# SiLU as one ScalarE operation in a hybrid attention, state-space and feed-forward layer

## The chip, the cores and the metric

The kernel runs on one core of a Trainium2 chip. The core has a matrix engine (TensorE, PE in the profile, with its weight loads shown as PEld), a vector engine (VectorE, DVE), a scalar engine (ScalarE, ACT), a general engine (GpSimd, POOL) and queues of transfers that SyncE (SP) starts. Each engine works through its own queue of instructions in order and waits where an instruction needs another engine's result or a free buffer. The metric is the time of one launch on the device, in microseconds (us), as the median of several runs.

## The reference

One layer of a decoder over 1024 positions of width 1024, all in float32. What matters here is where a sigmoid, and where a SiLU, silu(a) = a * sigmoid(a), is computed:

```python
h = rms_norm(x, g_pre_mix)
q, k, v, z, xbc, dt_raw, ga, gs = _split(h @ w_in, IN_SIZES)
o_att = stick_breaking_attention(q, k, v)      # beta = sigmoid(q.k / sqrt(d)), causal
...
xbc = silu(conv4(xbc) + conv_b)                # 3072 channels, 4 taps over time
xs, bm, cm = _split(xbc, (2048, 512, 512))
y = ssd_chunked(xs * dt, dt * a, bm, cm) + d_skip * xs
y = y * silu(z)                                # 2048 channels
...
merged = sigmoid(ga) * (o_att @ w_br_att) + sigmoid(gs) * (o_ssm @ w_br_ssm)
x = x + rms_norm(merged @ w_mix_out, g_post_mix)
...                                            # cross-attention into 256 memory tokens
gate, up = _split(h @ w_gu, (2816, 2816))
x = x + rms_norm((silu(gate) * up) @ w_down, g_post_ffn)
```

The SSD (state-space) part and the cross-attention use exponentials, `dt` a softplus by exponential and logarithm.

## The kernel before, in words

**Products.** Each operand of a matrix product is split into a high and a low part: ACT rounds the high part off (`hi_sb`, L97), VectorE subtracts it for the low part (`lo_of`, L100), and PE makes three matmuls (high by high, high by low, low by high: L103 to L105 in `mm3`, L223 to L225 in `acc3`). Weights come from memory by transfers (`wr`, `wraw`), are added to one another where the block schemes of Strassen and Winograd want sums (POOL, L199 to L202, `sf`), and are split into `sw`, which PE reads. A pair of column blocks takes seven such products in place of eight (`winograd_weights`, `winograd_pair`), their sums being formed in `y` by ACT and VectorE (L233 to L244, L710).

**Stages**, with the time in the profiled span at which each runs:

- 0 to 82 us: norm of `x`, first products of `v` and `z` (`v_out`, `z_out`).
- 82 to 272: the rest of `v` and `z` with positions on the partitions (`put_v`, `put_z`). In `put_z`, `zo` is the block of z that goes to memory; its sums `zk`, `zu`, `ma` are made at L613 to L621.
- 272 to 660: x, B and C with channels on the partitions, by pairs of 128-channel blocks (`pair`). For each block `conv` takes the first tap and the bias by one ACT operation (L668), the other three taps by VectorE (L670), then the SiLU (L671, L672), and `tail` turns the result by PE transposes (L660) that ACT copies out (L662). Pairs of merge gates (`gate`, a Sigmoid at L681) are strewn among the twelve pairs of `conv` by a sorted list, roughly one after every two.
- 640 to 1070: stick-breaking attention. ACT takes the Sigmoid of the scores (L881), VectorE scans them (L882), PE transposes (L898), ACT and VectorE split the weights (L901, L902).
- 1070 to 1410: SSD in chunks of 128 positions: a product gives the decays' exponents (`dec`, L1072), ACT their Exp (L1073), VectorE masks and multiplies them (L1074), PE multiplies by the chunk (`pd`, L1124, eight heads) and makes the states (`pst`), VectorE adds `pd` (L1127). Until about 1210 the keys and values of the memory are projected between the chunks (weights `wraw`, split into `bw`, products `mm` at L103 to L105).
- 1410 to 1880: branch projections, mix, cross-attention.
- 1880 to 1950: entry of the feed-forward: two blocks by plain products (`standard`), while VectorE makes the operands of the Strassen scheme (`combos`, L1748 to L1773).
- 1950 to 2310: the feed-forward's gate and up products in pairs; `gated` makes silu(gate) * up for 128 channels and 512 positions (Sigmoid L1728, product by the gate L1729, product by `up` L1730) and sends it to memory.
- 2310 to 2540: down projection and last norm.

**What sets the order.** The program is written as one function and run through a planner that lays every instruction on a simulated timeline (`schedule_with_timeline_sim=True`, L2051) and writes each engine's queue in the order that this timeline gives. An edit in one place thus changes the order in others. Tile pools give buffers in turn (nine for `sw`, six of PSUM, the matmul results' memory, in the convolution stage), and an instruction waits until its buffer's last reader is done. Function tables of ACT are not in the source: an ACT_TABLE_LOAD is put ahead of an activation whose function is not in the set loaded last. Sigmoid, Silu, Exp and Ln are in different sets in this program; Copy and Identity need no load.

Of the kernel before, what the change touches and what calls it, by code (L numbers as in the profile page):

```python
# [11 lines left out]
AF = mybir.ActivationFunctionType  # L12
ALU = mybir.AluOpType
# [22 lines left out]
def hybrid_block(ctx, tc, a, out, dbg=None):  # L36
    nc = tc.nc
    V, A, G, T = nc.vector, nc.scalar, nc.gpsimd, nc.tensor
# [11 lines left out]
    def mk(pl, shape, dt, tag, bufs=None):  # L50
        uid[0] += 1
        kw = {} if bufs is None else {"bufs": bufs}
        return pl.tile(shape, dt, tag=tag, name=f"{tag}_{uid[0]}", **kw)
# [87 lines left out]
    def pcol(nm, k):  # L141
        c = P + rows[nm] + k
        return prmT[:, c:c + 1]

    def cw(t, f):
        return prmT[:, t * 24 + f:t * 24 + f + 1]
# [107 lines left out]
    with ExitStack() as pa:  # L254
# [55 lines left out]
        with ExitStack() as p1:  # L310
# [87 lines left out]
                nc.sync.dma_start(v_d[1 + c * P:1 + (c + 1) * P, i * HALF:(i + 1) * HALF], to)  # L398

            def z_out(c, i, x, to):  # L400
                A.activation(to, x, AF.Sigmoid)
                V.tensor_tensor(to, x, to, ALU.mult)
                nc.sync.dma_start(zs_d[c * P:(c + 1) * P, i * HALF:(i + 1) * HALF], to)

            def u_kept(ps):
# [34 lines left out]

            load_v, steps_v = ahead(C_V, v_out, u_kept)
            load_z, steps_z = ahead(C_Z, z_out, u_away)
            normed(0)
            normed(1)
# [27 lines left out]
        with ExitStack() as p1:  # L472
# [11 lines left out]
            def put_z(c, i, x):  # L484
                if c % 2 == 0:
                    two["t"] = mk(op, [P, S], F32, "zo")
                sg = two["t"][:, c % 2 * HALF:(c % 2 + 1) * HALF]
                A.activation(sg, x, AF.Sigmoid)
                V.tensor_tensor(sg, x, sg, ALU.mult)
                nc.sync.dma_start(zs_d[c * P:(c + 1) * P, i * HALF:(i + 1) * HALF], sg)  # L490

            def put_v(c, i, x):
# [130 lines left out]

            token_major(0, C_V, put_v, 0, True)
            token_major(1, C_Z, put_z, 0, True, dt_chain())
            token_major(2, C_Z + 2 * HALF, put_z, 2)
        pz.close()

# [8 lines left out]
        with ExitStack() as p1:  # L637
# [28 lines left out]
            def conv(f, y):  # L666
                acc = mk(t4, [P, S], F32, "b4")
                A.activation(acc, y, AF.Identity, scale=cw(3, f), bias=pcol("conv_b", f))  # L668
                for sh in (1, 2, 3):
                    V.scalar_tensor_tensor(acc[:, sh:], y[:, :S - sh], cw(3 - sh, f), acc[:, sh:], ALU.mult, ALU.add)  # L670
                A.activation(y, acc, AF.Sigmoid)  # L671
                V.tensor_tensor(acc, acc, y, ALU.mult)  # L672
                if 16 <= f < 20:
                    nc.sync.dma_start(bf_d[f - 16], acc)
                if f >= 20:
                    nc.sync.dma_start(cf_d[f - 20], acc)
                else:
                    pend.append((f, acc))
# [24 lines left out]
            def pair(c0, f, fin, npool, beside=()):  # L703
# [9 lines left out]
                for h in beside:  # L713
                    differences(h)()

            jobs = [(C_X + f * P, f, conv) for f in list(range(16, 24, 2)) + list(range(0, 16, 2))]
            gts = [(C_GA + f * P, f, gate) for f in range(0, 16 - LATE_GATES, 2)]
            order = [(-(-(i + 0.5) / len(l)), n, j) for n, l in enumerate((jobs, gts)) for i, j in enumerate(l)]
# [255 lines left out]
    acc = []  # L974
# [505 lines left out]
    with ExitStack() as q2:  # L1480
# [28 lines left out]
        def cols(t, c):  # L1509
            return t[:, :, c * P:(c + 1) * P]  # L1510
# [27 lines left out]
        for c in range(4):  # L1538
            x, y, z = cols(d1, c), cols(q67, c), cols(q45, c)
# [177 lines left out]
    with ExitStack() as q4:  # L1717
# [7 lines left out]
        def gated(f, half, gate, up):  # L1725

            sg = mk(t2, [P, HALF], F32, "t2")
            A.activation(sg, gate, AF.Sigmoid)  # L1728
            V.tensor_tensor(sg, sg, gate, ALU.mult)  # L1729
            V.tensor_tensor(sg, sg, up, ALU.mult)  # L1730
            nc.sync.dma_start(gu_d[f * P:(f + 1) * P, half * HALF:(half + 1) * HALF], sg)

        def standard(f):
            ws = wgu if f == 0 else [wq_load(rp, "wr", colblock(w_gu, c0 + f * P)) for c0 in (0, FFN)]
            for half in range(2):
                gate, up = pre if f == half == 0 else [proj(w, hf[half]) for w in ws]
                gated(f, half, gate, up)
# [8 lines left out]
        def whole(pair, k, eng):  # L1746
            t = mk(t2, [P, HALF], F32, "t2")
            eng.tensor_tensor(t, pair[0][:, k, :].bitcast(F32), pair[1][:, k, :].bitcast(F32), ALU.add)  # L1748
            return t
# [21 lines left out]
        for k in range(4):  # L1771
            x21, x = whole(b21, k, V), whole(t2_, k, V)
# [5 lines left out]
        def strassen(f):  # L1778
            def loads(r, kh):
                for b in range(2):  # L1780
                    yield r[:, :, b], w_gu[kh * 512:(kh + 1) * 512, b * FFN + f * P:b * FFN + (f + 1) * P].rearrange("(k p) f -> p k f", p=P)

            y = [[mk(t2, [P, HALF], F32, "t2"), mk(t2, [P, HALF], F32, "t2")], [None, mk(t2, [P, HALF], F32, "t2")]]
            p = winograd_pair(psp, winograd_weights(rp, sfp, swp, loads), hw, y)
            gated(f, 0, y[0][0], p)
            gated(f, 1, y[0][1], y[1][1])
# [268 lines left out]
```

## Time and profile before

| what | value |
|---|---|
| median of 3 runs | 2538.93 us (2537.61 to 2540.65) |
| profiled execution, own time | 2542.52 us |
| profiled execution, span (first to last instruction) | 2540.8 us |
| instructions | 32839 |
| busy: PE, DVE, ACT, POOL | 97%, 73%, 46%, 31% |
| mean granted PE clock | 0.996 |
| ACT_TABLE_LOADs | 9, each 1.28 us |

How to read it: busy shares are means over the whole span. A group's row gives engine, line, operation, the names of result and operands with their shapes, a count, busy us and mean ns of one, and then how long its engine stood idle before such instructions and on what it waited ("<-DVE sw L100": until VectorE's instruction of line 100 that writes `sw` was done). A row of the timeline begins with the start and the duration in us. The time of an execution is a little above its span, since the span begins with its first instruction.

### The profile page before, as it was taken

To read this page: it belongs to the slowest core of one execution; us is meant where nothing else is said; L and a number is where in the kernel's file an instruction comes from. 1 tells how busy PE (TensorE), PEld (TensorE's weight loads), DVE (VectorE), ACT (ScalarE), POOL (GpSimd) and SP (SyncE) were. 2 spreads that over 40 slices of the span, in tenths; PEclk is the share of its full clock that TensorE was granted. 3 is DMA by queue.
4 is the path that set the end of the run, shared out by engine and by line. 5 is a ranking of instruction groups with operands and counts; after the bars stand their busy time and mean duration, and the time that the engine had idled before them with its cause. 6 is when DMAs were issued, how large, how long until landed. Compare 5 with 4: busy or idle time off the path is not lost.

```text
span 2540.8 us, 32839 instructions
## 1 busy us (share of the span) xinstructions
PE 2473.5 (97%) x12002; PEld 2053.7 (81%) x12002; DVE 1856.2 (73%) x2197; ACT 1156.7 (46%) x2071; POOL 791.5 (31%) x629
## 2 busy tenths in 40 slices
PE   7999999999999999998999999999999999999998
PEld 6788788888888888787888788887887888887776
DVE  7686878776688887687888654576458666666997
ACT  6343455655555555565554302344333333334433
POOL 4331533331000000165655231131123233233675
PEclk9999999999999999999999999999999999999999
DMA  6441565445454453464332452321131322324322
GB/s 229 150 152 61 153 200 182 137 139 158 116 129 113 118 128 103 143 207 152 102 94 81 160 162 87 121 90 64 62 121 59 97 78 75 99 84 166 133 100 100
DMA packets 285996, 311.59 MB, mean 123 GB/s; under 512 B 17407, under 2 KB 205960, under 8 KB 285450
## 3 DMA queue, kind: packets, MB, share of 16 engines
q1 hardware_dynamic: 285834, 309.49, 39.2%
q8 instruction: 95, 1.56, 0.2%
q14 instruction: 67, 0.55, 0.1%
HBM read 206.26 MB, written 78.52 MB: 112 GB/s over the span
## 4 chain that ended last, share of the span: by engine, by line
PE 42%; DVE 6%; issue 1%; POOL 1%; DMA 1%; ACT 1%; SPq 0%; POOLq 0%; DVEq 0%; ACTq 0%
PE mm L225 5%; PE mm L223 5%; PE mm L224 5%; PE mm L103 4%; PE mm L104 4%; PE mm L105 4%; DVE op L100 2%; PE p L103 2%; PE p L104 2%; PE p L105 2%; PE pd L1124 2%; DVE a L1931 1%; PE p L1639 1%; DMA gr<-gu_d 1%; PE tr L181 0%
## 5 line engine op out<-in xcount | busy, mean ns | idle before, releaser
L882 DVE TENSOR_TENSOR_SCAN n<-n,mask 128x128 f32<-128x128 f32 (+7 forms) x128 | 170.8, 1350 | 39.9 <-ACT n L881 39.4
L199 POOL TENSOR_TENSOR sf<-wr,wr 128x512 f32<-128x512 f32 x38 | 61.4, 1617 | 354.6 <-DMA wr<-in_w_gu_dram 105.5
L100 DVE TENSOR_TENSOR sw<-sf,sw 128x512 fp32r<-128x512 f32 x150 | 114.5, 775 | 55.1 <-ACT sw L97 54.7
L93 POOL TENSOR_SCALAR whi<-wraw 128x1024 fp32r<-128x1024 f32 x10 | 18.3, 1829 | 397.8 <-PE mm L104 324.7
L97 ACT ACTIVATE sw<-sf 128x512 fp32r<-128x512 f32 x150 | 92.0, 625 | 96.2 <-PE mm L225 85.7
L881 ACT ACTIVATE n<-sc 128x512 f32<-128x512 f32 (+1 forms) x192 | 86.8, 493 | 93.6 <-PE sc L880 93.1
L97 ACT ACTIVATE sw<-wr 128x512 fp32r<-128x512 f32 x113 | 70.9, 629 | 123.4 <-PE mm L225 123.3
L225 PE MATMUL mm<-h,sw 128*128 128x512 f32 x320 | 125.0, 392 | 1.8 <-DVE sw L100 1.8
L223 PE MATMUL mm<-h,sw 128*128 128x512 f32 x320 | 122.6, 391 | 3.1 <-ACT h L97 2.3
L224 PE MATMUL mm<-h,sw 128*128 128x512 f32 x320 | 125.2, 391 | 0.0
L166 POOL TENSOR_SCALAR rstd<-ms 128x1 f32<-128x1 f32 x82 | 31.5, 384 | 294.6 <-ACT x L1417 132.7
L902 DVE SCALAR_TENSOR_TENSOR wtl<-tr,wth 128x512 fp32r<-128x512 f32 x192 | 99.5, 545 | 29.8 <-ACT wth L901 29.4
L901 ACT ACTIVATE wth<-tr,mone 128x512 fp32r<-128x512 f32 x192 | 106.5, 582 | 23.9 <-PE tr L898 21.7
L670 DVE SCALAR_TENSOR_TENSOR b<-b,prmT,b 128x1023 f32<-128x1023 f32 (+2 forms) x72 | 102.2, 1420 | 9.8 <-ACT b L668 9.2
L100 DVE TENSOR_TENSOR sw<-wr,sw 128x512 fp32r<-128x512 f32 x113 | 93.7, 832 | 19.0 <-ACT sw L97 18.9
L103 PE MATMUL mm<-oth,bw 128*128 128x512 f32 x256 | 104.1, 407 | 1.5 <-DVE a L1183 1.4
L105 PE MATMUL mm<-oth,bw 128*128 128x512 f32 x256 | 101.4, 396 | 0.5 <-DVE bw L1170 0.5
L898 PE MATMUL tr<-ident,n 128*128 128x128 f32 x576 | 97.9, 275 | 3.4 <-DVE wtl L902 3.4
L104 PE MATMUL mm<-otl,bw 128*128 128x512 f32 x256 | 101.0, 394 | 0.0
L103 PE MATMUL p<-bw,h 128*128 128x512 f32 x256 | 99.7, 390 | 0.9 <-DVE m L1391 0.9
L100 DVE TENSOR_TENSOR zl<-zr,zh 128x512 fp32r<-128x512 f32 x84 | 75.4, 911 | 34.4 <-ACT zh L97 34.3
L105 PE MATMUL p<-bw,h 128*128 128x512 f32 x256 | 100.2, 392 | 0.0
(697 smaller groups left out, 8202.6 us busy)
## 6 DMA issues: line engine op xcount, KB each, us to landing
wr<-in_w_gu_dram SPq DMA_DIRECT2D x80, 256.0 KB
wr<-in_w_in_dram SPq DMA_DIRECT2D x36, 512.0 KB
zr<-in_w_in_dram SPq DMA_DIRECT2D x32, 512.0 KB
gu_d<-t SPq DMA_DIRECT2D x44, 256.0 KB
qk<-hT SPq DMA_DIRECT2D x84, 128.0 KB
qk<-lT SPq DMA_DIRECT2D x84, 128.0 KB
wraw<-in_w_in_dram SPq DMA_DIRECT2D x20, 512.0 KB
b<-v_d SPq DMA_DIRECT2D x16, 512.0 KB
```

Source lines behind the costliest of these rows:

```text
L97: A.activation(o, i, AF.Copy)
L100: eng.tensor_tensor(o, i, hi.bitcast(F32), ALU.subtract)
L103: first = T.matmul(ps, sh, mh, start=start, stop=False)
L104: T.matmul(ps, sh, ml, start=False, stop=False)
L105: T.matmul(ps, sl, mh, start=False, stop=stop)
L223: T.matmul(ps, w[0][:, k, :], b[0][:, k, :], start=first and k == 0, stop=False, skip_group_check=True)
L224: T.matmul(ps, w[0][:, k, :], b[1][:, k, :], start=False, stop=False, skip_group_check=True)
L225: T.matmul(ps, w[1][:, k, :], b[0][:, k, :], start=False, stop=last and k == 3, skip_group_check=True)
L670: V.scalar_tensor_tensor(acc[:, sh:], y[:, :S - sh], cw(3 - sh, f), acc[:, sh:], ALU.mult, ALU.add)
L882: V.tensor_tensor_scan(nt[:, 0:L][:, ::-1], nt[:, 0:L][:, ::-1], mask[:, S - L:][:, ::-1], 1.0, ALU.mult, ALU.max)
L901: A.activation(wh[:, t0 * P:], pt[:, t0 * P:], AF.Identity, bias=mone)
L902: V.scalar_tensor_tensor(wl[:, t0 * P:], pt[:, t0 * P:], -1.0, wh[:, t0 * P:].bitcast(F32), ALU.add, ALU.subtract)
```

## The change

In `z_out`, `put_z`, `conv` and `gated` the pair of Sigmoid on ACT and product on VectorE becomes one Silu on ACT. In `conv` the result goes into `acc` itself, and `y` is no longer written there.

```diff
             def z_out(c, i, x, to):
-                A.activation(to, x, AF.Sigmoid)
-                V.tensor_tensor(to, x, to, ALU.mult)
+                A.activation(to, x, AF.Silu)
                 nc.sync.dma_start(zs_d[c * P:(c + 1) * P, i * HALF:(i + 1) * HALF], to)
...
                 sg = two["t"][:, c % 2 * HALF:(c % 2 + 1) * HALF]
-                A.activation(sg, x, AF.Sigmoid)
-                V.tensor_tensor(sg, x, sg, ALU.mult)
+                A.activation(sg, x, AF.Silu)
                 nc.sync.dma_start(zs_d[c * P:(c + 1) * P, i * HALF:(i + 1) * HALF], sg)
...
                 for sh in (1, 2, 3):
                     V.scalar_tensor_tensor(acc[:, sh:], y[:, :S - sh], cw(3 - sh, f), acc[:, sh:], ALU.mult, ALU.add)
-                A.activation(y, acc, AF.Sigmoid)
-                V.tensor_tensor(acc, acc, y, ALU.mult)
+                A.activation(acc, acc, AF.Silu)
...
             sg = mk(t2, [P, HALF], F32, "t2")
-            A.activation(sg, gate, AF.Sigmoid)
-            V.tensor_tensor(sg, sg, gate, ALU.mult)
+            A.activation(sg, gate, AF.Silu)
             V.tensor_tensor(sg, sg, up, ALU.mult)
```

The other Sigmoids (`gate` L681, the late gates L858, the scores L881) stay. The changed file is shorter by a line at each place, so its line numbers are lower by one to four: L681 is L678, L671 is L669, L881 is L878, L1072 is L1069, L1124 is L1121, L1728 is L1725.

The queues change in three places that matter. First VectorE's queue between z and the convolution (about 270 us; `zu` are sums of z, `zo` the block of z that is sent, `sw` the split weights of the convolution's first pair). Before:

```order
L621 TENSOR_TENSOR zu_2044<-zu_2044,ma_2272 128x512
L621 TENSOR_TENSOR zu_2046<-zu_2046,ma_2273 128x512
L621 TENSOR_TENSOR zu_2048<-zu_2048,ma_2274 128x512
L489 TENSOR_TENSOR zo_2517<-zu_2044,zo_2517 128x512
L621 TENSOR_TENSOR zu_2050<-zu_2050,ma_2275 128x512
L489 TENSOR_TENSOR zo_2517<-zu_2046,zo_2517 128x512
L489 TENSOR_TENSOR zo_2526<-zu_2048,zo_2526 128x512
L100 TENSOR_TENSOR sw_2597<-wr_2582,sw_2597 128x512
L100 TENSOR_TENSOR sw_2598<-sf_2587,sw_2598 128x512
L489 TENSOR_TENSOR zo_2526<-zu_2050,zo_2526 128x512
```

And with the change:

```order
L619 TENSOR_TENSOR zu_2028<-zu_2028,ma_2252 128x512
L619 TENSOR_TENSOR zu_2030<-zu_2030,ma_2253 128x512
L619 TENSOR_TENSOR zu_2032<-zu_2032,ma_2254 128x512
L619 TENSOR_TENSOR zu_2034<-zu_2034,ma_2255 128x512
L100 TENSOR_TENSOR sw_2565<-wr_2550,sw_2565 128x512
L100 TENSOR_TENSOR sw_2566<-sf_2555,sw_2566 128x512
```

The products at L489 are gone, and the two splits follow the last sum directly.

Second, ACT's queue in the convolution stage, from a gate to the next convolved block (`b` are the blocks `y` and `acc`). Before:

```order
L681 ACTIVATE b_486_2760<-b_486_2760 128x1024
L97 ACTIVATE b_500_2902<-b_500_2902 128x8x64
L237 ACTIVATE b_515_2946<-mm_2948 128x512
L97 ACTIVATE sw_3076<-wr_3059 128x512
L97 ACTIVATE sw_3247<-wr_3235 128x512
L668 ACTIVATE b_520_3042<-b_515_2946,prmT_93 128x1024
L97 ACTIVATE sw_3248<-sf_3239 128x512
L97 ACTIVATE sw_3249<-sf_3240 128x512
L97 ACTIVATE sw_3250<-wr_3236 128x512
L671 ACTIVATE b_515_2946<-b_520_3042 128x1024
L97 ACTIVATE sw_3251<-sf_3241 128x512
```

And with the change:

```order
L678 ACTIVATE b_486_2726<-b_486_2726 128x1024
L237 ACTIVATE b_515_2912<-mm_2914 128x512
L97 ACTIVATE sw_3040<-wr_3023 128x512
L97 ACTIVATE sw_3209<-wr_3197 128x512
L666 ACTIVATE b_520_3008<-b_515_2912,prmT_93 128x1024
L97 ACTIVATE sw_3210<-sf_3201 128x512
L97 ACTIVATE sw_3211<-sf_3202 128x512
L97 ACTIVATE sw_3212<-wr_3198 128x512
L669 ACT_TABLE_LOAD
L669 ACTIVATE b_520_3008<-b_520_3008 128x1024
L97 ACTIVATE sw_3213<-sf_3203 128x512
```

A table load has come between the weight conversions and the SiLU of `conv`, and another stands ahead of the next pair of gates. In the whole program there are 21 loads in place of 9; eleven of the twelve new ones are of this kind, and one stands ahead of the first Sigmoid of the attention's scores.

Third, PE's queue near 1075 us, where the SSD's chunks and the memory's projections share PE (`dec` the decays, `pst` the states, `pd` the products with a chunk, `mm` the memory's products). Before:

```order
L1072 MATMUL dec_10338<-colrows_2076_10225,keyrows_2077_10226 128x512
L103 MATMUL mm_10369<-a_2073_10195,bw_10355 128x256
L104 MATMUL mm_10369<-a_2074_10196,bw_10355 128x256
L1072 MATMUL dec_10341<-colrows_2076_10225,keyrows_2077_10226 128x512
L103 MATMUL pst_10481<-s2r_10347,bh_10299 128x512
L104 MATMUL pst_10481<-s2r_10348,bh_10299 128x512
L105 MATMUL pst_10481<-s2r_10347,bl_10300 128x512
L105 MATMUL mm_10369<-a_2073_10195,bw_10355 128x256
```

And with the change:

```order
L1069 MATMUL dec_10282<-colrows_2076_10169,keyrows_2077_10170 128x512
L1069 MATMUL dec_10285<-colrows_2076_10169,keyrows_2077_10170 128x512
L1121 MATMUL pd_10460<-s_2102_10261,s_2103_10263 128x96 x6
L103 MATMUL pst_10425<-s2r_10291,bh_10243 128x512
L1121 MATMUL pd_10460<-s_2102_10261,s_2103_10263 128x96
L1121 MATMUL pd_10460<-s_2102_10261,s_2103_10263 128x64
L104 MATMUL pst_10425<-s2r_10292,bh_10243 128x512
L105 MATMUL pst_10425<-s2r_10291,bl_10244 128x512
L103 MATMUL mm_10313<-a_2073_10139,bw_10299 128x256
L104 MATMUL mm_10313<-a_2074_10140,bw_10299 128x256
```

The decays and the `pd` products of the first chunk now stand ahead of the first memory product; before, `pd` came behind the first 26 of the memory's matmuls. Further on the memory's products come in other blocks between the chunks than before.

## The prediction

> **What bounds the kernel now.** I read the busy shares first, then the same shares by stage, and then the waits inside the stages where the share falls. The page's first part:
>
> ```profile
> PE 2473.5 (97%) x12002; PEld 2053.7 (81%) x12002; DVE 1856.2 (73%) x2197; ACT 1156.7 (46%) x2071; POOL 791.5 (31%) x629
> ```
>
> TensorE (PE) works 2473.5 of the span's 2540.8 us. Whatever happens on VectorE (DVE) and ScalarE (ACT), no more than 2540.8 - 2473.5 = 67.3 us of PE idle time can be closed, beside time lost to a lowered clock. By stage (start and end, length, then busy us of PE, PEld, DVE, ACT and POOL, granted clock, DMA share, GB/s):
>
> ```profile
> 82.00:272.00 190.00, 189.82 (x835) 156.06 (x833) 129.78 (x183) 74.26 (x122) 50.90 (x26) 1.00 0.37 122
> 272.00:660.00 388.00, 382.87 (x1759) 315.53 (x1759) 302.29 (x316) 212.07 (x323) 119.10 (x74) 1.00 0.52 158
> 1070.00:1210.00 140.00, 123.19 (x727) 105.69 (x727) 113.37 (x122) 85.58 (x153) 79.80 (x69) 0.97 0.58 183
> 1880.00:1950.00 70.00, 65.22 (x273) 52.31 (x272) 62.02 (x79) 24.81 (x42) 26.14 (x15) 0.95 0.18 57
> 1950.00:2310.00 360.00, 359.22 (x1585) 297.25 (x1584) 230.20 (x269) 131.74 (x226) 106.91 (x68) 1.00 0.28 86
> ```
>
> The stages in which the change takes work from VectorE are 82 to 272 (z), 272 to 660 (convolution) and 1880 to 2310 (feed-forward). PE idles 0.2, 5.1, 4.8 and 0.8 us in the four rows that cover them. The 16.8 idle us of 1070 to 1210 hold no edited line.
>
> **What is removed.** A product and a Sigmoid become one Silu. The columns of a group are its count, then busy us and mean ns of one, then the engine's idle time before them and its releaser:
>
> ```profile
> L1729 DVE TENSOR_TENSOR t<-t,t 128x512 f32<-128x512 f32 x40 | 59.9, 1498 | 1.9 <-ACT t L1728 1.7
> L672 DVE TENSOR_TENSOR b<-b,b 128x1024 f32<-128x1024 f32 x24 | 37.1, 1546 | 4.9 <-ACT b L671 4.8
> L1730 DVE TENSOR_TENSOR t<-t,mm 128x512 f32<-128x512 f32 x24 | 16.5, 687 | 33.6 <-PE mm L225 31.3 <-PE mm L105 2.3
> L489 DVE TENSOR_TENSOR zo<-zk,zo 128x512 f32<-128x512 f32 x16 | 20.1, 1297 | 0.0
> L489 DVE TENSOR_TENSOR zo<-zu,zo 128x512 f32<-128x512 f32 x8 | 7.7, 996 | 0.0
> L489 DVE TENSOR_TENSOR zo<-ma,zo 128x512 f32<-128x512 f32 x4 | 2.7, 692 | 0.0
> L1729 DVE TENSOR_TENSOR t<-t,mm 128x512 f32<-128x512 f32 x4 | 2.7, 685 | 4.6 <-ACT t L1728 4.6
> L402 DVE TENSOR_TENSOR early<-ma,early 128x512 f32<-128x512 f32 x4 | 2.5, 684 | 0.6 <-ACT early L401 0.6
> ```
>
> Without L1730, which stays, these are 40+24+16+8+4+4+4 = 100 products and 59.9+37.1+20.1+7.7+2.7+2.7+2.5 = 132.7 us of VectorE, 7% of its work. L1730 shows why most of it buys nothing: the product by `up`, which follows L1729, has waited 33.6 us in all, nearly all for PE's matmuls. L1729 runs while PE is still making `up`.
>
> **What is added.** One ACT activation stands where one stood. No Silu is in this trace, so its duration is bounded by neighbours of the same size: a Sigmoid of 128x512 and a plain conversion.
>
> ```profile
> L1728 ACT ACTIVATE t<-t 128x512 f32<-128x512 f32 x40 | 25.3, 632 | 9.6 <-DVE t L244 3.9 <-DVE t L240 2.8
> L97 ACT ACTIVATE sw<-sf 128x512 fp32r<-128x512 f32 x150 | 92.0, 625 | 96.2 <-PE mm L225 85.7 <-POOL sf L200 4.4 <-POOL sf L202 2.4
> ```
>
> They differ by 7 ns, so I take no difference; the bound above is a Silu as dear as Sigmoid and conversion together, 0.63 us more apiece. In the feed-forward that is less than the L1729 that it replaces.
>
> Function tables are the second addition. The instruction order of the change holds 21 ACT_TABLE_LOADs, that of before 9. All 12 new ones lie in the convolution (11, because Silu of `conv` and Sigmoid of `gate` take turns) and at the first score of the attention (1). Their price:
>
> ```profile
> 462.01 1.28 ACT L671 ACT_TABLE_LOAD   x1 [0.51 <-DVE b L670]
> 463.30 1.06 ACT L671 ACTIVATE b<-b 128x1024 f32<-128x1024 f32 x1
> ```
>
> The activation starts 1.29 us after its load, so a switch costs 1.29 us of ACT, and it stands behind the wait for the data: the load does not run ahead of it. 12 x 1.29 = 15.5 us. The Trainium skill, page "ScalarE: Activation LUTs", sections "What ACT_TABLE_LOAD costs" and "Table sets: the hidden batching unit", tells authors to batch calls by table set and charges each switch a drain of about 1380 ns beside the load's 1283 ns, 2.66 us together. That rule speaks against this change. The row agrees on the load and shows no drain; by the page the twelve would be 31.9 us (an estimate from its figure), still ACT time.
>
> **The sum, place by place.**
>
> *z to convolution, 270 to 277 us.* VectorE's queue and PE's wait:
>
> ```profile
> 271.74 3.44 DVE L489 TENSOR_TENSOR zo<-zu,zo 128x512 f32<-128x512 f32 x2
> 275.10 1.76 DVE L100 TENSOR_TENSOR sw<-wr,sw 128x512 fp32r<-128x512 f32 x1
> 272.99 0.50 PE L225 MATMUL mm<-b11h,sw 128*128 128x512 f32 x1 [0.77 <-POOL sw L100]
> 276.92 0.50 PE L225 MATMUL mm<-b21h,sw 128*128 128x512 f32 x1 [1.36 <-DVE sw L100]
> ```
>
> Two z products, 3.44 us, stand directly ahead of the weight split for which PE waits 1.36 us. In the new order the four `zu` products are gone and the split moves up. The wait ends: **-1.4 us**. Bounds: 0 if the split finds its input late, -2.1 if the neighbour's 0.77 goes too.
>
> *Convolution.* What waits for what, in total us, times, and longest:
>
> ```profile
> PE tr L660 <- DVE b L672: 0.7, 2, 0.4
> ACT sw L97 <- PE mm L225: 42.2, 30, 5.4
> ACT b L710 <- PE mm L225: 38.9, 17, 4.1
> ACT b L671 <- DVE b L670: 21.5, 18, 4.5
> ```
>
> PE has waited 0.7 us for the removed product and so can win that much. The loads lengthen ACT by 11 x 1.29 = 14.2 us, to 226 of 388. Queued behind a load are weight conversions (L97), for which PE waits if they come late. But ACT itself idles for PE 42.2 + 38.9 us in this stage, so most loads end inside its slack. Each convolved block also loses a 1.55 us product and gains a 1.29 us load at most, so the transposes get their data no later. I take **0**; bounds -0.7 and +14.2 (no load covered).
>
> *First score of the attention.* One load stands ahead of it:
>
> ```profile
> 665.71 0.56 ACT L881 ACTIVATE n<-sc 128x128 f32<-128x128 f32 x2 [1.75 <-PE sc L880]
> 671.03 0.49 PE L898 MATMUL tr<-ident,n 128*128 128x128 f32 x3
> ```
>
> PE needs what comes of it 5.3 us later and multiplies other things until then: **0**, at most +1.29.
>
> *1070 to 1210.* No line here is edited, but the planner puts PE's queue in another order: four decays and eight `pd` products stand ahead of the first memory product, where they came after it. The largest waits:
>
> ```profile
> PE mm L103 <- ACT bw L97: 2.9, 1, 2.9
> PE po L104 <- DVE stl L100: 2.2, 1, 2.2
> PE pd L1124 <- DVE s L1127: 2.1, 3, 1.0
> PE dec L1072 <- ACT cb L1048: 2.1, 1, 2.1
> ```
>
> The new order puts work in front of the 2.9 us wait for memory weights, so that row could go. But eight `pd` products now come together, and the third row, their wait for the addition (L1127) that empties their buffer of the chunk before, could grow by as much. I take **0**. Bounds: -16.8 (all idle time of the stage) and +8.7 (a wait as long as the longest, 2.9, at each of the three places where the blocks of memory products are cut differently).
>
> *Entry of the feed-forward.* The only stretch where VectorE never rests:
>
> ```profile
> 1920.00:1930.00 10.00, 7.68 (x31) 5.95 (x30) 10.00 (x18) 4.17 (x8) 0.00 (x0) 0.92 0.03 8
> 1926.56 0.68 DVE L1729 TENSOR_TENSOR t<-t,mm 128x512 f32<-128x512 f32 x1
> 1926.76 0.50 PE L223 MATMUL mm<-h,sw 128*128 128x512 f32 x1 [2.31 <-ACT h L97]
> 1927.16 0.69 DVE L1759 TENSOR_TENSOR t<-t,t 128x512 f32<-128x512 f32 x1
> 1927.76 0.68 DVE L1729 TENSOR_TENSOR t<-t,mm 128x512 f32<-128x512 f32 x1
> 1930.00:1940.00 10.00, 8.01 (x28) 5.83 (x27) 10.00 (x18) 3.65 (x7) 2.45 (x1) 0.84 0.33 107
> 1937.53 0.50 PE L225 MATMUL mm<-h,sw 128*128 128x512 f32 x1 [1.82 <-DVE sw L100]
> ```
>
> Two L1729 stand in that queue ahead of the split for which PE waits 1.82 us. Each gives back one pitch, 1927.16 - 1926.56 = 0.60 us by their neighbours (L1729, then L1759, then L1729: 1.20 for two): **-1.2 us**. Bounds: 0 if the time goes to other operands, -4.1 if both waits (2.31 + 1.82) go, and up to 10 x (0.08 + 0.16) = 2.4 us more for the clock that fell behind them.
>
> *All else.* z at 82 to 272 and the feed-forward at 1950 to 2310 have PE busy in 189.82 of 190 and 359.22 of 360 us: **0**, with 0.2 + 0.8 = 1.0 us as the most that could be won. If that cover went, it would be the 132.7 us.
>
> Sum: -1.4 + 0 + 0 + 0 - 1.2 + 0 = -2.6 us on the profiled span of 2540.8. The profiled execution took 2542.5 in its own time, 1.7 more than its span, and lies 3.6 above the median of the runs, 2538.93. The difference carries over: 2538.9 - 2.6 = **2536.3 us**.
>
> **Rivals.**
>
> *A, the relief compounds.* The gap at the entry closes with its clock loss (-4.1 - 2.4), the transition gives 2.1, and the new order of 1070 to 1210 hides a quarter of its idle time (4.2): -12.8, or 2526. For it: the clock falls right behind the waits, and the 16.8 us lie in a region that is re-planned. Against it: nothing edited lies there. If only some of this comes, 2530.
>
> *B, the table switches decide.* Slower: 11 loads stand ahead of conversions that PE needs; the slack of ACT comes in pieces (42.2 us in 30 waits, 1.4 each, hardly more than one load), and an ACT that runs late makes PE wait by what is over. It decides once more than two loads' worth (2.6 us, the sum above) shows on PE, and is slower by more than 5.1 us once 6 of the 11 do. With 8 exposed: 2538.9 - 2.6 + 10.3 = 2547; all of them and the attention's: 2536.3 + 15.5 = 2552. Against it: ACT is busy 212 of 388 us. Charged as that page charges a switch, all twelve exposed would be 2568 (an estimate).
>
> *C, the new order costs.* Slower: the three places between 1070 and 1210 each gain a wait of 2.9 us: 2536.3 + 8.7 = 2545. For it: a planner's timeline is not the chip's. Against it: the stage has waits to lose too.
>
> *D, nothing.* PE's own order of work keeps the waits, each removed product's time going to the next operand in line: 2539.
>
> **How the numbers follow.** Forecast, small gain: 0.46. A 0.26, B 0.10, C 0.11, D 0.07. The forecast's own range is 2532 to 2540: its two gains at their bounds (-2.1 and -4.1, so 2532.7) and one exposed load above (2537.6), with some for the spread of the runs (2537.6 to 2540.7). The range of 8 in 10 takes in the middle of A, all of C and B up to eight exposed loads: 2525 to 2547; outside lie the far ends of A and of B. About 0.2%, or 5.1 us, is what a measurement can tell from no change: faster is below 2533.8, slower above 2544.0. A gives 0.24 of faster and the forecast's low end 0.06; B gives 0.09 and C 0.09 of slower; the rest is same, 0.52.
>
> **What would show each step.** In the changed profile: the wait of 1.36 us near 277 us gone; PE idle in 272 to 660 no more than 5.1 us with 11 loads in ACT's groups, each 1.28 us (B: new waits of PE on `sw` from ACT, about 1.3 us each); VectorE less by 120 to 133 us; PE busy unchanged near 2473; the stage 1950 to 2310 the same length; the waits at 1926 and 1937 us shorter by 1.2 in all. The forecast is wrong if the stage from convolution to attention grows by several us (B), or if 1070 to 1210 changes by more than 4 us either way (A or C): then the planner's order, and not the removed products, made the time.

## The result, and the profile after

The change takes 2531.97 us (median of 15 runs, 2528.16 to 2535.96) against 2538.93 for the kernel before (15 runs, 2536.68 to 2541.19): a ratio of 0.9972 with a 95% interval of 0.9966 to 0.9979, that is 5.3 to 8.6 us or 0.28% faster. The forecast was 2.6 us. The profiled execution took 2533.23 us, with a span of 2531.5.

The busy shares, from the page of the changed kernel:

```profile
PE 2471.4 (98%) x12002; PEld 2054.0 (81%) x12002; DVE 1745.0 (69%) x2097; ACT 1168.9 (46%) x2083; POOL 791.0 (31%) x629
```

A hundred instructions have left VectorE, and ACT has its twelve loads. TensorE's work is the same, so what was won is its idle time and its clock. The same stages as in the prediction, by time (columns as there; the last stages begin earlier now):

```profile
272.00:660.00 388.00, 384.42 (x1769) 317.63 (x1770) 265.32 (x289) 224.59 (x335) 113.56 (x74) 1.00 0.51 158
1070.00:1210.00 140.00, 127.82 (x754) 110.19 (x752) 115.28 (x125) 86.75 (x158) 78.93 (x72) 0.98 0.60 181
1880.00:1950.00 70.00, 67.24 (x287) 54.88 (x288) 60.50 (x80) 26.33 (x46) 38.11 (x15) 0.98 0.23 72
1950.00:2310.00 360.00, 359.22 (x1586) 297.11 (x1585) 189.46 (x227) 132.85 (x229) 104.02 (x67) 1.00 0.29 91
```

In the last row VectorE has 40.7 us less to do (230.20 before) and PE's 359.22 is unchanged to the hundredth: there the removed products were worth nothing. PE gains 1.6 us in the convolution, 4.6 from 1070 to 1210, and 2.0 at the entry of the feed-forward. Fixed windows shift against the work, though, so the stages are better cut at instructions that both kernels have. The entry runs from the last transposes of the normed stream to the first product of the Strassen scheme that uses `tx`. TensorE's timeline of before, and then of the change:

```profile
1884.97 1.03 PE L181 MATMUL tr<-ident,x 128*128 128x128 f32 x8
1949.71 0.39 PE L223 MATMUL mm<-tx,sw 128*128 128x512 f32 x1
```

```profile
1878.64 1.03 PE L181 MATMUL tr<-ident,x 128*128 128x128 f32 x8
1939.43 0.39 PE L223 MATMUL mm<-tx,sw 128*128 128x512 f32 x1
```

64.74 us have become 60.79: 3.95 us in this one place. The convolution stage, from its first product to the attention's first score, of before and of the change:

```profile
270.04 0.39 PE L223 MATMUL mm<-b11h,sw 128*128 128x512 f32 x1
665.22 0.39 PE L879 MATMUL sc<-qk 128*128 128x128 f32 x2
```

```profile
270.47 0.39 PE L223 MATMUL mm<-b11h,sw 128*128 128x512 f32 x1
663.60 0.39 PE L876 MATMUL sc<-qk 128*128 128x128 f32 x2
```

395.2 us have become 393.1. The SSD stage, cut in the same way (from the last attention product, `av`, to the last product of the state branch, `mm<-otl,bw`), went from 382.9 to 378.0; how much of that is the change's, the experiments have to say. These three cuts, in every kernel that was profiled (lengths in us, taken from the starts of the matmuls named; "entry" here from the last of the eight transposes):

| kernel | convolution | SSD | entry | ratio to before (95% interval) |
|---|---|---|---|---|
| before, the profile of the prediction | 395.2 | 382.9 | 64.0 | 1 |
| before, profiled again (e12) | 394.7 | 376.7 | 64.0 | 1 |
| the change | 393.1 | 378.0 | 60.0 | 0.9972 (0.9966 to 0.9979) |
| e1, last four z blocks | 395.2 | 375.6 | 62.6 | 0.9998 (0.9989 to 1.0007) |
| e2, the rest of z | 394.2 | 377.4 | 63.9 | 1.0000 (0.9991 to 1.0009) |
| e3, the change without the 11 switches | 393.1 | 376.9 | 60.0 | 0.9967 (0.9955 to 0.9980) |
| e4, feed-forward alone | 394.0 | 378.5 | 59.9 | 0.9985 (0.9977 to 0.9994) |
| e5, convolution alone | 394.8 | 382.9 | 63.9 | 1.0020 (1.0011 to 1.0028) |
| e6, z and convolution | 393.1 | 378.1 | 64.0 | 0.9993 (0.9984 to 1.0002) |
| e7, z and feed-forward | 395.8 | 376.3 | 60.6 | 0.9992 (0.9983 to 1.0000) |
| e8, first two feed-forward blocks alone | 394.2 | 377.3 | 59.3 | 0.9984 (0.9975 to 0.9993) |
| e9, the change, entry refilled | 393.3 | 377.9 | 64.0 | 0.9987 (0.9978 to 0.9996) |
| e10, the change, entry emptied further | 393.1 | 377.9 | 59.7 | 0.9970 (0.9959 to 0.9982) |
| e11, the change, 37 more loads | 404.0 | 376.9 | 60.6 | 1.0012 (1.0003 to 1.0020) |

0.001 of the ratio is 2.5 us. The lengths are those of one execution each, the ratio that of all runs. The profiled executions of e1 (2533.94 us) and e8 (2532.09) were the fastest of their eleven, and a stretch that no run edits, from the last product of gate and up to the end, lasted between 230.0 and 235.2 us.

### The profile page after: what moved, and what is told of

Same layout as the page of the kernel before. It is cut to its first block, busy times and chain, and to the rows that moved or that the text cites. A ratio compares the mean times of both kernels' runs of the same rounds, so it can differ in the third digit from the quotient of the medians.

```text
span 2531.5 us, 32776 instructions
## 1 busy us (share of the span) xinstructions
PE 2471.4 (98%) x12002; PEld 2054.0 (81%) x12002; DVE 1745.0 (69%) x2097; ACT 1168.9 (46%) x2083; POOL 791.0 (31%) x629
## 5 line engine op out<-in xcount | busy, mean ns | idle before, releaser
L879 DVE TENSOR_TENSOR_SCAN n<-n,mask 128x128 f32<-128x128 f32 (+7 forms) x128 | 170.8, 1350 | 40.7 <-ACT n L878 40.1
L199 POOL TENSOR_TENSOR sf<-wr,wr 128x512 f32<-128x512 f32 x38 | 70.6, 1858 | 335.8 <-DMA wr<-in_w_in_dram 150.5
L878 ACT ACTIVATE n<-sc 128x512 f32<-128x512 f32 (+1 forms) x192 | 86.8, 493 | 93.0 <-PE sc L877 92.6
L100 DVE TENSOR_TENSOR sw<-wr,sw 128x512 fp32r<-128x512 f32 x113 | 107.3, 953 | 24.7 <-ACT sw L97 24.7
```

Source lines behind the costliest of these rows:

```text
L100: eng.tensor_tensor(o, i, hi.bitcast(F32), ALU.subtract)
L879: V.tensor_tensor_scan(nt[:, 0:L][:, ::-1], nt[:, 0:L][:, ::-1], mask[:, S - L:][:, ::-1], 1.0, ALU.mult, ALU.max)
```

## The experiments

### Is the gain in the places that the trace shows? (e1 to e4)

The two theories at the start were P, three places (the end of z, the new order of the SSD stage, the entry of the feed-forward), and W, that all of VectorE's work counts alike; beside them the rival L, that the table loads cost PE something. z was cut in two, because its last four blocks stand at the transition and decide which order the planner gives the SSD stage.

**e1, the last four z blocks alone.**

```diff
             def put_z(c, i, x):
...
-                A.activation(sg, x, AF.Sigmoid)
-                V.tensor_tensor(sg, x, sg, ALU.mult)
+                if i == 3 and c < 4:
+                    A.activation(sg, x, AF.Silu)
+                else:
+                    A.activation(sg, x, AF.Sigmoid)
+                    V.tensor_tensor(sg, x, sg, ALU.mult)
```

> Silu only in four blocks of z, the last ones ahead of the convolution (in put_z for i = 3 and c below 4); everything else as before, so 4 of the 100 products go, about 4 us of VectorE. Theory P (three places make the gain: the end of z, the planned order of 1070 to 1210, the entry of the feed-forward): this removes the products at the first place, and the planner then writes PE's queue from 1070 to 1210 as in the change, so both of these gains come and the third does not: 1.6 + 5 = 6.6 faster, 2532 to 2534. Theory W (every us of VectorE taken away is worth the same, 7.0 us for 132.7): 0.2 faster, 2538.7.

Measured: 2538.01 against 2537.99, ratio 0.9998. P fell in two of its three places. The wait at 277 us is gone, as it should be; what PE waits for in the convolution now (TensorE's waits of e1 from 268 to 660 us; the lines are three higher in its file than in the kernel before):

```profile
PE tr L663 <- DVE b L675: 1.1, 2, 0.7
PE mm L223 <- ACT b L237: 1.1, 1, 1.1
PE mm L225 <- DVE sw L100: 0.9, 1, 0.9
```

Before it was 1.4 + 0.8 at the transition and 0.7 at the transposes. The transition gave 1.2, but the transposes wait 0.4 more for the convolved product (L675 here, L672 before), and a wait of 1.1 for an ACT result is new: the stage is 395.2 us, as in the profile of before. And although e1 has the change's order in the SSD stage (375.6 us), its median does not move. Its entry, which it does not edit, is 62.6 us long in this profile and not 64.0; the section on the hardware comes back to that.

**e2, the rest of z** (the complement: `z_out`, and `put_z` but for those four blocks).

```diff
             def z_out(c, i, x, to):
-                A.activation(to, x, AF.Sigmoid)
-                V.tensor_tensor(to, x, to, ALU.mult)
+                A.activation(to, x, AF.Silu)
...
             def put_z(c, i, x):
...
+                if not (i == 3 and c < 4):
+                    A.activation(sg, x, AF.Silu)
+                else:
+                    A.activation(sg, x, AF.Sigmoid)
+                    V.tensor_tensor(sg, x, sg, ALU.mult)
```

> The complement within z: Silu in z_out and in put_z but for those four blocks, so 28 products, some 28.6 us of VectorE, go; the order of PE's queue is that of before throughout. Theory P: no gain, 2538 to 2540. Theory W: 28.6 x 7.0 / 132.7 = 1.5 faster, 2537.4.

Measured: ratio 1.0000 (0.9991 to 1.0009), so no gain from 28 products; W's 1.5 us lies inside the interval too. What its trace adds: with the order of before it takes 377.4 us in the SSD stage, not 382.9.

**e3, the change without the switches of table in the convolution.**

```diff
             def gate(f, y):
-                A.activation(y, y, AF.Sigmoid)
+                A.activation(y, y, AF.Copy)
```

> The change, with the gates' Sigmoid in the convolution stage (gate) replaced by a Copy of the same size, which needs no table: the gates are left without their sigmoid, 11 of the 12 added table loads go (14.1 us of ACT), PE's order is that of the change. Theory P (loads are hidden in ACT's slack): as the change, 2531 to 2533. Rival L (loads cost PE and were paid for by other gains): faster than the change, by 2 us if two are exposed, up to 14: 2518 to 2530.

Measured: ratio 0.9967 against the change's 0.9972, intervals overlapping. The median, 2530.10, lies between L's range and P's, so the time alone does not decide; but the stage is 393.1 us in both. The eleven loads cost nothing that can be seen there.

**e4, the feed-forward alone.**

```diff
         def gated(f, half, gate, up):
...
-            A.activation(sg, gate, AF.Sigmoid)
-            V.tensor_tensor(sg, sg, gate, ALU.mult)
+            A.activation(sg, gate, AF.Silu)
             V.tensor_tensor(sg, sg, up, ALU.mult)
```

> Silu only in the feed-forward's gating, 44 products and 62.6 us of VectorE; z and convolution as before, and so is PE's order until the feed-forward. Theory P: the third gain alone, 4 us by the trace, part of it given back in the down projection (1 us): 2535 to 2536. Theory W: 62.6 x 7.0 / 132.7 = 3.3 faster, 2535.6. The two agree on the time; the trace tells them apart by where it falls: P has 4 us between 1915 and 1945 us and nothing from 1950 to 2310, W a steady gain over 1950 to 2310.

Measured: ratio 0.9985, 3.7 us faster (1.5 to 5.8). The entry is 59.9 us, the 20 Strassen blocks, from the first product of `tx` to the start of their last, 359.9 us as in the kernel before. So the gain lies where P has it, and W falls.

### What do z and the convolution bring together, and which products count? (e5 to e8)

**e5, the convolution alone.**

```diff
             def conv(f, y):
...
-                A.activation(y, acc, AF.Sigmoid)
-                V.tensor_tensor(acc, acc, y, ALU.mult)
+                A.activation(acc, acc, AF.Silu)
```

> Silu only in the convolution, so 24 products and 37.1 us of VectorE go and the added table loads come (22 in all); z and feed-forward as before; PE's queue from 1070 to 1210 is neither that of before nor that of the change. What the feed-forward's edit (3.7 faster alone) and z's edit (0.0 alone) leave of the 7.0 is 3.3. Theory J (joint: the 1.1 to 1.6 us won at the end of z is given back within the convolution unless its products go as well): alone this wins at most 1 us in the convolution, 2537 to 2538, or anything within 3 of it by the third order of 1070 to 1210. Theory S (the convolution alone holds the 3.3): 2534 to 2535. Rival L (the loads cost): slower, from 2541.

Measured: 2543.15, ratio 1.0020 (1.0011 to 1.0028): slower by 5.1 us; all of its eleven runs (2542.08 to 2545.66) lie above before's median. J and S both missed it, and it is not L: the convolution is 394.8 us long with its loads. Its profile has the loss in the SSD stage, 382.9 us; this kernel's third order of that stage. PE's waits there, from 1060 to 1215 us (lines lower by one than before's):

```profile
PE dec L1071 <- ACT cb L1047: 3.7, 2, 2.7
PE po L104 <- DVE stl L100: 2.2, 1, 2.2
PE dec L1071 <- DMA keyrows<-key_d: 1.2, 1, 1.2
```

The wait for `cb` is 3.7 us in two where before had one of 2.1. That the loss is real is shown by eleven runs; that it lies here rests on one profile, and one profile of before was as long here, so the place is likely, not shown.

**e6, z and convolution** (both edits above, the feed-forward as before).

> Silu in z and in the convolution, the feed-forward as before: PE's queue is that of the change up to the feed-forward, with all its table loads. Theories J and S both: 3.3 faster, 2534 to 2535; the trace keeps about 2 us up to 640 us, and the entry of the feed-forward takes 64 us as before, not 60. If the sum of the parts were no sum (the entry pays more when it is reached in another state), 2537 or 2531.

Measured: 2537.18, ratio 0.9993 (0.9984 to 1.0002): 1.8 us faster, less than the 3.3 expected, with an interval that holds that, and nothing. The convolution is 393.1 us and the entry 64.0.

**e7, z and feed-forward**, the convolution as before.

> Silu in z and in the feed-forward, the convolution as before, so without the 12 switches of table; PE's queue from 1070 to 1210 is that of the change. Theory J: z's gain is given back in the convolution, the feed-forward's stays: 3.7 faster, 2534 to 2535, so 3 slower than the change. Rival L (loads cost PE): faster than the change, under 2531.

Measured: 2536.45, ratio 0.9992 (0.9983 to 1.0000): 2.1 us faster where J expected 3.7 (the interval, 0 to 4.3, holds both), and slower than the change, whose interval it does not touch. Taking out the convolution's edit, with its twelve loads, makes the kernel worse, and the stage 395.8 us long. With e1, e5 and e6 the lengths of the stage fit J: the transition's products gone but not the convolution's, 395.2 and 395.8; the convolution's alone, 394.8; both, 393.1 to 393.3 in five profiles; neither (e2 and e4 among them), 394.0 to 395.2 in five. The times of e1, e6 and e7 are too close to one another to confirm it.

**e8, the first two feed-forward blocks alone** (4 of 44 products).

```diff
         def gated(f, half, gate, up):
...
+            if f < NSTD:
+                A.activation(sg, gate, AF.Silu)
+            else:
+                A.activation(sg, gate, AF.Sigmoid)
+                V.tensor_tensor(sg, sg, gate, ALU.mult)
-            A.activation(sg, gate, AF.Sigmoid)
-            V.tensor_tensor(sg, sg, gate, ALU.mult)
             V.tensor_tensor(sg, sg, up, ALU.mult)
```

> Silu only in the first two blocks of the feed-forward (standard, f below 2): 4 of the 44 products there, 2.7 us of VectorE, go; the other 40 (59.9 us) stay. Theory P (only the entry counts, where VectorE never rests): all of the feed-forward's gain, the entry 60 us and not 64, 2534 to 2535. Theory W (work counts): 2.7 x 3.65 / 62.6 = 0.2 faster, 2537.8.

Measured: 2534.43, ratio 0.9984 (0.9975 to 0.9993), 4.1 us faster. Four products, 2.7 us of VectorE, are worth all that the feed-forward's 44 are; the 40 others (59.9 us) nothing.

### Why are four products worth 4 us? (e9, e10) How much cover have the loads? (e11) Was the first profile a fair one? (e12)

**e9, the entry refilled.**

```diff
             A.activation(sg, gate, AF.Silu)
+            if f < NSTD:
+                V.tensor_tensor(sg, sg, sg, ALU.max)
             V.tensor_tensor(sg, sg, up, ALU.mult)
```

> The change, with one VectorE operation of the same size put back in each half of the first two feed-forward blocks (the maximum of the gated value with itself, which alters nothing, in place of the product by the gate); Silu stays. PE's queue there is, but for a few rows, that of the kernel before. Theory P (VectorE's time at the entry is what PE waits for): the entry takes 64 us again and the whole 4 more than the change, 2536 to 2537. Rival A (the shorter way through ACT alone, Silu in one step, made the gain): entry 60, 2532.

Measured: ratio 0.9987, 3.7 us of the change's gain lost, the entry 64.0 us. PE's waits in it are those of before again, 2.30 and 1.78 us for 2.31 and 1.82:

```profile
1919.75 0.50 PE L223 MATMUL mm<-h,sw 128*128 128x512 f32 x1 [2.30 <-ACT h L97]
1930.52 0.50 PE L225 MATMUL mm<-h,sw 128*128 128x512 f32 x1 [1.78 <-DVE sw L100]
```

So it is VectorE's queue there that counts, not the shorter way through ACT. The planner answers to the refilled queue with PE's old order as well, so the freed time and the new order could not be taken apart.

**e10, the entry emptied further.**

```diff
             A.activation(sg, gate, AF.Silu)
-            V.tensor_tensor(sg, sg, up, ALU.mult)
+            if f >= NSTD:
+                V.tensor_tensor(sg, sg, up, ALU.mult)
```

> The change, with the product by up also left out in the first two blocks of the feed-forward (these 256 channels are then silu(gate) alone), so that four more VectorE operations of 0.69 us go from the entry. If every operation taken from this queue is worth as much as the first four (4 us): entry 56, 2528. If the gain was the closing of one wait that is closed now: entry 60 to 58, 2530 to 2532.

Measured: ratio 0.9970, entry 59.7: as the change. Four more operations taken out bring nothing. PE's only long wait there, of the change and then of e10:

```profile
1924.53 0.50 PE L225 MATMUL mm<-a,sw 128*128 128x512 f32 x1 [2.54 <-DVE sw L100]
```

```profile
1925.59 0.50 PE L225 MATMUL mm<-a,sw 128*128 128x512 f32 x1 [2.23 <-DVE sw L100]
```

The wait hardly shrinks. But the queue ahead of it was not emptied either. What VectorE does from the last transpose to the end of this wait, in the change and then in e10 (length, then busy us and number of operations):

```profile
1879.41:1924.53 45.12, 40.34 (x54) 1.00 0.22 70
```

```profile
1879.89:1925.59 45.70, 41.77 (x54) 1.00 0.20 63
```

The planner put other operations in the place of the four, so that 54 stand there in both, and they take 1.4 us more. So e10 agrees with a gain that is a step, but it does not show one: a queue that is shorter at this wait was not tried.

**e11, 37 more loads.**

```diff
+            onec = mk(pool(p1, "onec"), [P, 1], F32, "onec")
+            G.memset(onec, 0.0)
...
+                A.activation(onec, acc[:, S - 1:S], AF.Sigmoid)
                 A.activation(acc, acc, AF.Silu)
```

> The change, with a Sigmoid of one column of the block (its result is read by nothing) ahead of each of the 24 Silu of the convolution, so that 57 table loads stand where 21 did: 36 x 1.28 = 46 us more of ACT in the convolution, 271 of 388, beside 24 very short activations. Theory P (ACT's slack hides loads): the convolution grows by 0 to 3 us, 2532 to 2535. Rival L (a load delays what stands behind it and PE with it): by a third of them or more, 15 us, from 2547; by all, 2578.

Measured: 2542.40, ratio 1.0012, so 10 us slower than the change, and the convolution 404.0 us instead of 393.1, 10.9 more. What ACT has to do for it (groups of ACT in e11: the loads ahead of the Silu, ahead of the small Sigmoid and ahead of the gates, and the small Sigmoid itself):

```profile
L672 ACT ACT_TABLE_LOAD x24 | 30.8, 1283 | 0.4
L671 ACT ACT_TABLE_LOAD x19 | 24.4, 1283 | 20.9 <-DVE b L670 20.7
L681 ACT ACT_TABLE_LOAD x6 | 7.7, 1283 | 0.1
L671 ACT ACTIVATE onec<-b 128x1 f32<-128x1 f32 x24 | 4.9, 203 | 10.3 <-DVE b L670 10.1
```

That is 49 loads where the change has 12, so 37 more (one more than was counted beforehand), 47.5 us, and 4.9 us of small activations. Where they went shows in ACT's waits for PE, of the change and then of e11:

```profile
ACT sw L97 <- PE mm L225: 41.8, 36, 3.0
ACT b L707 <- PE mm L225: 30.7, 15, 3.7
ACT b L237 <- PE mm L225: 17.2, 10, 2.2
```

```profile
ACT sw L97 <- PE mm L225: 24.6, 25, 2.5
ACT b L710 <- PE mm L225: 12.3, 8, 2.8
ACT b L237 <- PE mm L225: 11.7, 6, 2.2
```

89.7 us of slack have become 48.6: 41.1 of the 52.4 us were swallowed, and the other 11.3 are about what the stage grew by (10.9). (ACT's busy and idle time make up the stage, so this says only that its other waits changed little in all.) The growth lies between what P (0 to 3) and L (15 or more) expected. PE's new waits (2.1 and 3.1 us at the longest) are for ACT:

```profile
PE tr L660 <- ACT b L672: 4.1, 3, 2.1
PE mm L223 <- ACT b L710: 3.6, 2, 3.1
```

So rival L's mechanism exists, with a price that begins only when the slack is used in places; the change's eleven are well within it.

**e12, the kernel before, profiled again.**

> The kernel before once more, for a second profile. If the profile used for the prediction was an execution that was slow between 1070 and 1410 us (three kernels with the same order there take 4 to 5 us less), this one takes 313 to 315 from the end of the attention to the last state product, not 319, and its own time is 2537 to 2539. If the order of before is slow there in itself, 319 again.

Measured: 2538.27 us, and 312.5 us from the end of the attention to the last state product, where the first profile had 318.9. The same stretch, 1070 to 1410 us, of the first profile of before and then of the second:

```profile
1070.00:1410.00 340.00, 323.15 (x1826) 276.88 (x1826) 282.52 (x333) 188.75 (x354) 195.45 (x183) 0.98 0.42 127
```

```profile
1070.00:1410.00 340.00, 326.88 (x1853) 280.37 (x1852) 287.04 (x339) 190.83 (x356) 196.23 (x184) 0.99 0.43 134
```

The first was an execution that lost some 5 us here. Over the four other profiles with before's order the SSD stage takes 377.5 us in the mean (376.7 to 378.5), over the eight with the change's order 377.2 (375.6 to 378.1). The new order is worth nothing that can be told from this spread; what looked like a gain of 4.9 us between two profiles was one execution's bad luck, whose cause is open.

No version better than the change came out of this: every part taken out of it cost time, or made no difference beyond the interval.

## Why the prediction was right, and where it was not

The direction held and the time lies inside the range (2525 to 2547), but below the likeliest case's own range (2532 to 2540) by a hair, and 7.0 us is 2.7 times the 2.6 of the sum. By its terms:

- **PE bounds, so most of the 132.7 us buy nothing.** Right: 40 products of the feed-forward are worth nothing (e8 against e4), 28 of z nothing (e2), PE in 1950 to 2310 is unchanged.
- **z to convolution, -1.4, and convolution, 0.** Together right, by another way: the stage with z's transition went from 394.5 (mean of the five profiles with before's order there) to 393.1, -1.4. But the two terms are not independent. The transition's gain alone is given back in the convolution (e1, e7: 395.2 and 395.8), in waits for convolved blocks and for one ACT result (e1); only with the convolution's own 24 products gone is it kept. The prediction did not ask what is late next after that wait.
- **Table loads, 0.** Right (e3), and for the reason given: ACT's slack. The price per load was right, 1.28 us, and none of the loads in `conv` and `gate` is followed by a drain: the activation starts 1.29 or 1.30 us after each. One of them, in the change's convolution, and then the load ahead of the attention's first score:

```profile
340.31 1.28 ACT L669 ACT_TABLE_LOAD   x1 [2.72 <-DVE b L668]
341.60 1.06 ACT L669 ACTIVATE b<-b 128x1024 f32<-128x1024 f32 x1
662.12 1.28 ACT L878 ACT_TABLE_LOAD   x1
664.32 0.56 ACT L878 ACTIVATE n<-sc 128x128 f32<-128x128 f32 x2 [0.92 <-PE sc L877]
```

"The load does not run ahead" of the wait for the data held in the convolution but not there: this load was over 0.92 us before the score came, and held up nothing.

- **Silu at the price of a Sigmoid.** Right: 24 of 128x1024 took 1060 ns each (Sigmoid 1061), 40 of 128x512 took 632 (632).

```profile
L669 ACT ACTIVATE b<-b 128x1024 f32<-128x1024 f32 x24 | 25.4, 1060 | 17.2 <-DVE b L668 17.2
L1725 ACT ACTIVATE t<-t 128x512 f32<-128x512 f32 x40 | 25.3, 632 | 10.9 <-DVE t L244 5.0 <-DVE t L240 2.8
```

- **SSD stage, 0.** Right (377.5 and 377.2), though the two profiles that were compared first seemed to refute it.
- **Entry of the feed-forward, -1.2.** This is the term that was mis-sized: it measured -4.0. It was counted as two pitches of 0.60 us off a busy queue. In the profile of before PE has three waits over 0.15 us in that queue, 2.31, 0.17 and 1.82, and two stretches at the lowered clock. In e12 the same kernel is as long, 64.0, but the matmuls after the first wait keep their speed, and PE then waits 1.57 in place of 0.17 for a split (`sw`). In both this wait ends 47.0 us after the last transpose. This wait in the profile of before, and then the first two waits of e12:

```profile
1932.71 0.50 PE L225 MATMUL mm<-a,sw 128*128 128x512 f32 x1 [0.17 <-DVE sw L100]
```

```profile
1921.65 0.50 PE L223 MATMUL mm<-h,sw 128*128 128x512 f32 x1 [2.31 <-ACT h L97]
1927.59 0.51 PE L225 MATMUL mm<-a,sw 128*128 128x512 f32 x1 [1.57 <-DVE sw L100]
```

So VectorE sets the time, and the first slow stretch only hides a wait. Against e12, which like the change has one slow stretch of eight matmuls, the waits went from 5.7 us to 2.5 (one wait of 2.54): 3.2 of the 4.0 us. Most of the rest goes with the number of waits, four in e12 with a small one and one in the change: beyond the wait itself, the matmul that waited and the next one start some 0.27 us late together. Against e12 the clock gives nothing. The prediction's bound for the waits, -4.1, was near; but its middle was the VectorE time saved, and it read 4.1 us of waits where 5.7 were VectorE's, since the slow stretch hid the third. Why 2.7 us less of VectorE's work end 3.2 us of waits is not shown: the planner's order changed with it, and several of the operations that stay take another time.

Terms as measured: -1.4 - 0.3 - 4.0 = -5.7, inside the interval (-5.3 to -8.6); the 1.3 us to the median are not assigned. VectorE lost 111.2 us and not 120 to 133, in part since operations that stay became slower: the weights' low parts took 107.3 us for 93.7, 13.6 of the 21.5 us that are missing.

```profile
L100 DVE TENSOR_TENSOR sw<-wr,sw 128x512 fp32r<-128x512 f32 x113 | 107.3, 953 | 24.7 <-ACT sw L97 24.7
```

Of the rivals, A had the entry too large (-4.1 - 2.4, and against e12 the clock gave nothing) by about as much as the sum had it too small, and the SSD stage wrong. B fell (e3), and would need some tens of loads more (e11). C fell for this change, but e5 may be of its kind: a third order, with no edit beyond the convolution, came with 5 us more. By the Trainium skill, page "ScalarE: Activation LUTs", section "Table sets: the hidden batching unit", the change does what its rule on batching by set warns of, twelve times; these runs agree that switches cost ACT time, and show that it reaches the total only beyond ACT's slack.

## What to carry to other kernels

In a kernel whose matrix engine is 97% busy, 100 removed vector operations brought 7 us. Four of them, in the one stretch where the vector engine never rests, brought 4, and the others a little at one transition. Size such a gain by the matrix engine's waits on that queue, the one that a slow stretch hides included, not by the time of the operations removed; and look for what gives it back in the stage after. Before explaining a difference between two profiles, profile the first kernel a second time: here a stage differed by 5 to 6 us between two executions of the same program.

## What the runs showed of the hardware

**Waits of about 2 us are often, not always, followed by a slow stretch.** From TensorE's timeline of before, after the wait at the entry (1926.76, quoted in the prediction):

```profile
1927.80 0.40 PE L223 MATMUL mm<-a,sw 128*128 128x512 f32 x1
1928.03 0.39 PE L224 MATMUL mm<-a,sw 128*128 128x512 f32 x1
1928.26 0.58 PE L225 MATMUL mm<-a,sw 128*128 128x512 f32 x1
...
1931.20 0.63 PE L225 MATMUL mm<-h,sw 128*128 128x512 f32 x1
1931.62 0.44 PE L225 MATMUL mm<-a,sw 128*128 128x512 f32 x1
1931.90 0.40 PE L223 MATMUL mm<-a,sw 128*128 128x512 f32 x1
```

Matmuls of one size go from 0.39 to 0.63 us, 1.5 us after the wait's end, and back 3.4 us later; in between they start every 0.42 us (eight in 3.36 us) and not every 0.23, so the eight take 1.5 us longer. Of the 19 waits of 1.8 to 2.5 us at the entry in these profiles, 14 were followed by such a stretch and five were not: the same wait of 2.31 in e12, 2.29 in e5, 2.49 in e8, and both of e1 (2.29 and 1.79), whose entry is 1.3 us shorter than that of before although nothing was edited there. The Trainium skill, page "TensorE: Matmul & The Clock Gate", section "What's actually happening", has the clock fall after an idle window of about 3.4 us; here waits of 1.8 to 2.5 us were enough in 14 of 19 cases, and the length of the slow stretch agrees with that window. What decides between the two was not tried.

**Side by side, now GpSimd is slow and now VectorE.** GpSimd's timeline of the change at the entry, the same sum of weights twice, and then VectorE beside the first and beside the second:

```profile
1892.12 1.30 POOL L199 TENSOR_TENSOR sf<-wr,wr 128x512 f32<-128x512 f32 x1 [5.04 <-DMA wr<-in_w_gu_dram]
1903.77 12.64 POOL L199 TENSOR_TENSOR sf<-wr,wr 128x512 f32<-128x512 f32 x1 [4.71 <-DMA wr<-in_w_gu_dram]
```

```profile
1892.31 1.66 DVE L100 TENSOR_TENSOR h<-t,h 128x512 fp32r<-128x512 f32 x1
1904.34 0.68 DVE L1755 TENSOR_TENSOR t<-t,t 128x512 f32<-128x512 f32 x1
```

1.30 us and 12.64. VectorE is busy without a pause beside both (10.00 of 10 us from 1905 to 1915), so that alone does not slow GpSimd. Beside the short sum VectorE's operation takes 1.66 us, beside the long one, from 1904 to 1915 us, its operations of this size take 0.68 or 0.69. So either engine can be the slow one; what decides which was not tried.
